# Products ahead of a norm for two outputs together and then one by one, and a shorter batch in the convolution's last projection

## The chip, the cores and the metric

The kernel runs on one core of a Trainium2 chip. The metric is the device time of one execution in microseconds (us). Engines are named as in the profile: PE is TensorE (matmuls; PEld its weight loads), DVE is VectorE, ACT is ScalarE, POOL is GpSimd, SP issues most of the DMAs.

## What is computed

A two-layer transformer block (first differential attention, then a gated short convolution as mixers, each followed by a gated feed-forward) and then a second block (a state-space branch, a pooling branch, a mixture of experts), on 256 tokens of width 1024 in 32-bit floats. What matters here is this pattern, which comes three times in the stretch that the change touches:

```python
h = rmsnorm(x, g) * (1.0 + scale) + shift      # x * rsqrt(mean(x*x) + eps) * g, then modulate
y = h @ w_in                                    # short conv: 3 parts; feed-forward: 2 parts; block 2: many
...
x = x + gate * (inner @ w_out)
mod = silu(c) @ ada_w + ada_b                   # shift, scale, gate of each layer ("adaLN")
```

The short convolution computes `(b_gate * conv(c_gate * u)) @ w_out` with `b_gate, c_gate, u = split(h @ w_in)`.

## The kernel before, in words

**Layout.** Activations lie with channels on the partitions: x is eight tiles of 128 channels by 256 tokens. An output of 128 channels is the sum over k of eight (or, behind a feed-forward, 22) products of 128 by 128 weight tiles with 128 by 256 activation tiles. Every operand is split in a high and a low half (`wh`, `wl` for weights, `hh`, `hl` for h), and each product is three matmuls (`mm3`, L277 to L282). A *unit* is eight weight tiles, 24 matmuls.

**Weights.** `Stream` loads them in order, two units a DMA (`fill`, L125), into a ring of four. `split_to` (L137) turns a unit into its halves: `wh` by a copy on ScalarE (L146), `wl` by a subtraction on VectorE (`lows`, L134), in a ring of five buffers; a buffer comes free when TensorE has used its unit up. `take(n, ahead)` (L175) hands out n tiles; for each unit that it starts it splits up to `ahead` units further on (3 where nothing is given) and calls `background`. `more(n)` splits up to n units from the present place.

**Order.** The program is written out in order by hand; each engine runs its instructions in the order in which the program issues them and waits for the others by semaphores. What is issued first on ScalarE or VectorE goes first there, ready or not.

**Background.** The modulation vectors are sums on VectorE, one instruction of 128 by 1024 for each 128 entries (`ada`, L395), from a queue of 128. `background` (L248) adds `bg_pace` (0.7, in the convolution's projections 0.25) to a counter at each unit and runs one sum for each whole number; while `hold` is set it does nothing. `need(key)` (L256) runs what is left up to a certain part at once.

**Residual.** `residual` (L886) computes the eight outputs of a projection; for each, VectorE adds it to x (L910), and `after` issues the square of x on ScalarE for the norm's sum (`sumsq_step`, L332; GpSimd adds the squares up) and, ahead of a raw entry, the split of A times x (`Raw.split`, on ScalarE and VectorE, L930 and L931). Outputs named in `done` were computed before, together, by `together` (L781): for the convolution's last projection four (L1131).

**Products ahead of the norm.** A norm multiplies a token's column by one number, so products with x can run before that number is known. `Raw` (L916) does this for the first outputs of the next stage; two more columns carry the shift. `Raw.run` (L942) goes through the eight k with all the outputs side by side: after the first k it sums the squares on TensorE (`total`, L351) and issues the chain of small VectorE instructions for the reciprocal root (`rstd`); after the third it turns it into rows (matmul L953) and copies them on ScalarE (`rows_s`, L956). The rest of the k follow, and then `modulated` (L971), which makes h for all other outputs by `norm_apply` (L371): for each k a VectorE instruction (`na`, L379), a ScalarE copy (`hh`, L380) and a VectorE subtraction (`hl`, L383). The raw outputs are finished by `lift` (L963).

It is used three times: at the convolution (three outputs, called from L1075), at the second feed-forward (four, L1008, after the convolution's last projection) and at the second block (four, L1201). There `dt_products` (L1179) runs small products at each k beside it, two streams of squares are summed (L1156 and L1157), and after it a list of steps written by hand (L1524) sets the order: lifts, splits, convolution steps, and `cb` (L1343), a product of two of the results.

Of the kernel before, what the change touches and what calls it, by code (L numbers as in the profile page):

```python
# [8 lines left out]
F32 = mybir.dt.float32  # L9
# [8 lines left out]
P = 128  # L18
T = 256
D = 1024  # L20
KD = 8
# [86 lines left out]
class Stream:  # L108
# [51 lines left out]
    def more(self, n, defer=False):  # L160

        self.fill(self.pos // 8 // 2 + self.ring)
        self.split_to(self.pos // 8 + n, defer)
# [74 lines left out]
class Builder:  # L238
# [93 lines left out]
    def sumsq_step(self, ms, xk, k, tag="rp_a", **kw):  # L332

        nc = self.nc
        sq = self.wk.tile([P, T], F32, tag=tag if k == 0 else "sq", name="sq", bufs=2)
        if k == 0:
            self.acc[tag] = sq
        nc.scalar.activation(sq, xk, AF.Square, **kw)  # L338
        if 0 < k < KD - 2:
            nc.gpsimd.tensor_tensor(self.acc[tag], self.acc[tag], sq, op=ALU.add)  # L340
        if k == KD - 2:
            self.acc[tag, 1] = sq
        if k == KD - 1:
            self.totals.append((ms, (self.acc[tag], self.acc[tag, 1], sq)))
# [80 lines left out]
def build(ctx, tc, ap):  # L425
    b = Builder(ctx, tc, ap)
# [24 lines left out]
    st = b.st = Stream(b, ap["ws"], ap["ws"].shape[0], ST, 5, 3)  # L451
# [103 lines left out]
    raw = ms[:, 16:16 + 4 * KD].rearrange("p (n a) -> p n a", a=4)  # L555
    rps = b.aux.tile([P, 512], F32, tag="aux", name="rows")

    def sums(src):

        acc = b.wk.tile([P, T], F32, tag="rp_a", name="acc", bufs=2)  # L560
        nc.scalar.activation(acc, src[0], AF.Square)
        for k in ks[1:]:
            sq = b.wk.tile([P, T], F32, tag="sq", name="sq", bufs=2)
            nc.scalar.activation(sq, src[k], AF.Square)
            if k < KD - 1:
                nc.vector.tensor_tensor(acc, acc, sq, op=ALU.add)
        return acc, sq
# [46 lines left out]
    for n in ks:  # L614
        w = st.raw()
# [68 lines left out]
    for n in range(8):  # L684
        w = st.take(KD)
        ps = b.ps.tile([P, 2, T], F32, tag="ps", name="ps_k") if n else \
# [10 lines left out]
    lo_, _ = VEC["lam"]  # L697
# [48 lines left out]
    for n in range(4):  # L746
        pss = [b.ps.tile([P, 2, T], F32, tag="ps", name="ps_v") for _ in range(2)]
        for half in range(2):
            wh, wl, _ = st.take(8)[0]
            wh = wh.rearrange("p (k a) c -> p k (a c)", a=2)  # L750
            wl = wl.rearrange("p (k a) c -> p k (a c)", a=2)
            for kk in range(4):
                k = half * 4 + kk
                for tt in range(4):
                    o = pss[tt // 2][:, tt % 2]
# [17 lines left out]
    def by_tiles(outs, xh, xl):  # L773

        w = st.take(KD * len(outs), 5 - len(outs))
        for k in range(KD):
            for i, o in enumerate(outs):
                b.mm3(o, w[i * KD + k], xh[:, k], xl[:, k], k == 0 and i % 2 == 0, k == KD - 1)
            yield

    def together(outs, xh, xl):  # L781
        for _ in by_tiles(outs, xh, xl):
            pass
        return outs
# [101 lines left out]
    def residual(ktiles, xh, xl, gate, sums, done=(), raw=None):  # L886


        pend = []

        def after():
            n = pend.pop(0)
            sums(n)
            if raw:
                raw.split(n)

        for n in range(KD):
            if n < len(done):
                ps = done[n]
            else:  # L900
                b.hold = raw is not None and n == KD - 1
                w = st.take(ktiles)
                ps = b.ps.tile([P, 512], F32, tag="ps", name="ps_r")[:, :T]
                for k in range(ktiles):
                    b.mm3(ps, w[k], xh[:, k], xl[:, k], k == 0, k == ktiles - 1)
                while pend:
                    after()
                if raw and n == KD - 1:
                    st.more(4)
            nc.vector.scalar_tensor_tensor(x[:, n], ps, gate[:, n:n + 1], x[:, n], op0=ALU.mult, op1=ALU.add)  # L910
            pend.append(n)
        after()
        if not raw:
            st.more(4, True)

    class Raw:  # L916
# [14 lines left out]
            nc.vector.scalar_tensor_tensor(self.L[:, n, :T], x[:, n], A, self.H[:, n, :T], op0=ALU.mult, op1=ALU.subtract)  # L931

        def steps(self, outs, more):
            w = st.take(KD * len(outs), 0)
            for k in range(KD):
                if more:
                    more(k)
                for i, o in enumerate(outs):
                    b.mm3(o[:, :T + 2], w[i * KD + k], self.H[:, k], self.L[:, k], k == 0, k == KD - 1)
                yield  # L940

        def run(self, rstd, outs, more=None):  # L942

            go = self.steps(outs, more)
            next(go)
            b.total()
            r = self.r = rstd()
            st.more(5 - len(outs))
            next(go)
            next(go)  # L950
            rows = self.rows_ps = b.aux.tile([P, 512], F32, tag="aux", name="rows")
            for tt in range(2):
                nc.tensor.matmul(rows[:, tt * P:(tt + 1) * P], lhsT=r[:, 2 * tt:2 * tt + 1].to_broadcast([P, P]),  # L953
                                 rhs=ident, start=(tt == 0), stop=True, skip_group_check=True)
            self.rows = b.wk.tile([P, T], F32, tag="rp_b", name="rows_s", bufs=2)
            nc.scalar.activation(self.rows, rows[:, :T], AF.Copy)  # L956
            for _ in go:
                pass
            hh, hl = modulated(self.rows, self.A, self.B)
            b.hold = False  # L960
            return hh, hl
# [9 lines left out]
    def modulated(rows, A, B):  # L971
        hh = hpool.tile([P, KD, T], F32R, tag="hh", name="hh", bufs=1)
        hl = hpool.tile([P, KD, T], F32R, tag="hl", name="hl", bufs=1)
        b.norm_apply([x[:, k] for k in ks], rows, A, B, [hh[:, k] for k in ks], [hl[:, k] for k in ks])
        return hh, hl
# [5 lines left out]

    ms = b.new_ms()
    residual(KD, oH, oL, mod(0, 2), lambda n: b.sumsq_step(ms, x[:, n], n), wo_out)
    b.ada_last = ada2
    b.ada_bufs = [w for w in b.ada_bufs if w is not ada2]
# [18 lines left out]
    def ffn(i, ms, sums, after, raw=None):  # L1004
# [39 lines left out]
        for j in range(2, KFF):  # L1044
            ps = b.ps.tile([P, 512], F32, tag="ps", name="ps_f")
            for a in range(2):
                w = st.take(KD)
                next(steps, None)
                project(w, ps[:, a * T:(a + 1) * T], hh, hl, a == 0)
                next(steps, None)  # L1050
            steps = glu(j, ps)
        for _ in steps:
            pass
        b.need((key, 5))
        u = after()
        residual(KFF, gH, gL, mod(i, 5), sums, (), u)
        fs.close()
        return u
# [19 lines left out]
    rH = cvp.tile([P, KD, T], F32R, name="rH")  # L1078
    rL = cvp.tile([P, KD, T], F32R, name="rL")
# [35 lines left out]
    for i in range(1, KD):  # L1115
        ps = b.ps.tile([P, 512], F32, tag="ps", name="ps_cu")
        pb = b.ps.tile([P, 512], F32, tag="ps", name="ps_b")
        for j, o in enumerate((ps[:, :T], ps[:, T:], pb[:, :T])):
            w = st.take(KD)
            next(steps, None)  # L1120
            project(w, o, hh, hl, j != 1)
            next(steps, None)
        for _ in steps:
            pass
        steps = conv(i, ps, pb)
# [2 lines left out]
        pass  # L1128
    b.bg_pace = 0.7
    b.need(("L1", 2))  # L1130
    pss = [b.ps.tile([P, 2, T], F32, tag="ps", name="ps_so") for _ in range(2)]  # L1131
    so_out = together([pss[i // 2][:, i % 2] for i in range(4)], rH, rL)
    ms2 = b.new_ms()
    raw3 = Raw(*ffn_in(1), yp, "yL")
    residual(KD, rH, rL, mod(1, 2), lambda n: b.sumsq_step(ms2, x[:, n], n), so_out, raw3)
    cs_.close()

# [278 lines left out]
    po, _ = CST["pinv"]  # L1416
# [272 lines left out]
    ro, _ = VEC["router_bias_2"]  # L1689
# [49 lines left out]
    for q in range(4):  # L1739
# [4 lines left out]
        for i in range(2):  # L1744
            k = 2 * q + i
# [7 lines left out]
    ro, _ = VEC["router_bias_2"]  # L1753
# [110 lines left out]
    ps = []  # L1864
# [281 lines left out]
    for i in range(4):  # L2146
        y, o, f = piece(i)
# [5 lines left out]
    for i, eng in ((0, nc.sync), (1, nc.scalar), (3, nc.sync), (2, nc.scalar)):  # L2153
        y, o, f = piece(i)
# [158 lines left out]
```

## Time and profile before

| | us |
|---|---|
| three runs | 1561.92, 1558.98, 1562.48 (median 1561.92) |
| the profiled execution | 1554.01 |
| its span in the trace | 1552.2 |
| TensorE busy in it | 1480.8 (95%), mean granted clock 0.988 |
| VectorE busy | 987.8 (64%) |
| ScalarE busy | 669.0 (43%) |

Times in a timeline are from the span's start. A timeline line gives start, duration, engine, line and operation, output and inputs by tile name, shape, and how many instructions it merges; in brackets stands how long the engine was idle before it and who ended that. Instructions overlap with their neighbours, so the distance of two starts, and not the duration, is what one costs in a row.

### The profile page before, as it was taken

The page shows a single profiled execution, that of the slowest core. Times are in us where ns is not written, and L with a number is a line of the kernel's source. Part 1 is how long each engine was busy: PE and PEld are TensorE (multiplying, and loading weights), DVE is VectorE, ACT ScalarE, POOL GpSimd, SP SyncE. Part 2 cuts the span into 40 slices and gives each one's busy share as a digit, 9 for nine tenths or more (in the row PEclk, how much of TensorE's full clock was granted, in tenths as well). Part 3 has the DMA queues.
Part 4 walks back from the last instruction along what each step waited for, and adds up shares of the span by engine and source line. Part 5 has one row for each costly group of instructions (what it writes and reads, how often), then busy time and mean ns, then how long its engine had stood idle before and what let it go on. Part 6 is the DMA issues. An engine that isn't in the chain of part 4 may idle for free. (4 is left out here: it accounts for less than half of the span.)

```text
span 1552.2 us, 28284 instructions
## 1 busy us (share of the span) xinstructions
PE 1480.8 (95%) x11184; PEld 1185.0 (76%) x11184; DVE 987.8 (64%) x1850; ACT 669.0 (43%) x1175; POOL 276.2 (18%) x439
## 2 busy tenths in 40 slices
PE   6999888999999999999899999999999999999996
PEld 5788578999999899999899998999634444444432
DVE  3698767888888789887888877465423333323332
ACT  3524554544455454454677765443322222222222
POOL 0170560000100100021067667001100000000000
PEclk9999999999999899999999999999999999999998
DMA  9678224987957569786444544667489999999995
GB/s 388 224 247 284 103 73 186 347 326 292 352 197 250 191 231 355 297 312 236 145 167 153 190 164 154 237 249 324 164 310 414 420 419 421 420 419 420 421 420 210
DMA packets 71429, 431.93 MB, mean 278 GB/s; under 512 B 8176, under 2 KB 8688, under 8 KB 28416
## 3 DMA queue, kind: packets, MB, share of 16 engines
q1 hardware_dynamic: 68656, 422.77, 71.0%
q0 software_dynamic: 1344, 4.80, 0.8%
q10 hardware_dynamic: 1296, 2.55, 0.5%
q8 instruction: 88, 1.44, 0.4%
q14 instruction: 45, 0.37, 0.1%
HBM read 429.01 MB, written 1.08 MB: 277 GB/s over the span
## 5 line engine op out<-in xcount | busy, mean ns | idle before, releaser
L134 DVE TENSOR_TENSOR wl<-st,wh 128x1024 fp32r<-128x1024 f32 x294 | 364.7, 1249 | 74.5 <-ACT wh L146 74.0
L146 ACT ACTIVATE wh<-st 128x1024 fp32r<-128x1024 f32 x294 | 306.2, 1055 | 113.2 <-PE ps_r L281 45.2
L280 PE MATMUL ps_f<-hh,wh 128*128 128x256 f32 x672 | 189.6, 282 | 2.5 <-ACT hh L380 2.1
L282 PE MATMUL ps_f<-hh,wl 128*128 128x256 f32 x672 | 189.5, 282 | 0.7 <-DVE wl L134 0.7
L281 PE MATMUL ps_f<-hl,wh 128*128 128x256 f32 x672 | 189.4, 282 | 0.1
L395 DVE SCALAR_TENSOR_TENSOR ada<-ada,crow 128x1024 f32<-128x1024 f32 x128 | 164.8, 1295 | 18.3 <-DMA ada<-in_ada 18.3
L340 POOL TENSOR_TENSOR sq<-sq 128x256 f32<-128x256 f32 x30 | 40.5, 1356 | 575.6 <-ACT sq L338 575.2
L280 PEld LDWEIGHTS ps_f<-hh,wh 128*128 128x128 f32 x672 | 127.6, 190 | 2.9 <-ACT hh L380 2.3
L282 PEld LDWEIGHTS ps_f<-hh,wl 128*128 128x128 f32 x672 | 127.5, 190 | 1.0 <-DVE wl L134 1.0
L281 PEld LDWEIGHTS ps_f<-hl,wh 128*128 128x128 f32 x672 | 127.6, 190 | 0.3 <-DVE hl L383 0.3
L280 PE MATMUL ps_ssd<-hh,wh 128*128 128x256 f32 x352 | 101.4, 288 | 0.0
L280 PE MATMUL ps_r<-gH,wh 128*128 128x256 f32 x352 | 98.7, 280 | 0.0
L281 PE MATMUL ps_r<-gL,wh 128*128 128x256 f32 x352 | 98.7, 280 | 0.0
L282 PE MATMUL ps_r<-gH,wl 128*128 128x256 f32 x352 | 98.7, 280 | 0.0
L282 PE MATMUL ps_ssd<-hh,wl 128*128 128x256 f32 x352 | 98.6, 280 | 0.0
L281 PE MATMUL ps_ssd<-hl,wh 128*128 128x256 f32 x352 | 98.6, 280 | 0.0
L1817 DVE TENSOR_SCALAR xb<-gtp,A,mod 128x256 f32<-128x256 f32 (+2 forms) x52 | 27.4, 526 | 111.5 <-ACT xb L1815 111.3
L1815 ACT ACTIVATE xb<-gtp,mod,A 128x256 f32<-128x256 f32 (+2 forms) x52 | 28.6, 551 | 118.6 <-PE gtp L1835 118.4
L1805 POOL TENSOR_TENSOR WG<-G,pwq 128x256 f32<-128x256 f32 (+2 forms) x24 | 14.1, 608 | 366.4 <-DVE G L1801 366.4
L274 ACT ACTIVATE oH<-wr 128x512 fp32r<-128x512 f32 (+2 forms) x53 | 33.4, 630 | 95.2 <-DVE wr L2093 82.6
L1835 PEld LDWEIGHTS gtp<-G,utH 128*128 128x128 f32 x208 | 39.2, 189 | 45.9 <-DVE xb L1817 19.7
L280 PEld LDWEIGHTS ps_ssd<-hh,wh 128*128 128x128 f32 x352 | 66.3, 188 | 1.0 <-issue 1.0
(616 smaller groups left out, 4156.0 us busy)
## 6 DMA issues: line engine op xcount, KB each, us to landing
st<-in_ws SPq DMA_DIRECT2D x151, 1024.0 KB, 6.0
ada<-in_ada SPq DMA_DIRECT2D x128, 512.0 KB, 5.0
w<-in_we SPq DMA_DIRECT2D x40, 1024.0 KB, 19.8
w_st<-in_we SPq DMA_DIRECT2D x40, 1024.0 KB, 19.8
w_y<-in_we SPq DMA_DIRECT2D x32, 1024.0 KB, 19.8
w_ut<-in_we SPq DMA_DIRECT2D x30, 1024.0 KB, 19.8
w_h<-in_we SPq DMA_DIRECT2D x21, 1024.0 KB, 19.8
x<-in_we SPq DMA_DIRECT2D x10, 1024.0 KB, 19.8
```

The source lines that it names most:

```text
L134: self.b.nc.vector.tensor_tensor(lo.rearrange("p a c -> p (a c)"), w, h.rearrange("p a c -> p (a c)"), op=ALU.subtract)
L146: nc.scalar.activation(h.rearrange("p a c -> p (a c)"), w, AF.Copy)
L274: self.nc.scalar.activation(h, src, AF.Copy)
L280: nc.tensor.matmul(out, lhsT=h[:, k], rhs=xh, start=start, stop=False, skip_group_check=True)
L281: nc.tensor.matmul(out, lhsT=h[:, k], rhs=xl, start=False, stop=False, skip_group_check=True)
L282: nc.tensor.matmul(out, lhsT=lo[:, k], rhs=xh, start=False, stop=stop, skip_group_check=True)
L340: nc.gpsimd.tensor_tensor(self.acc[tag], self.acc[tag], sq, op=ALU.add)
L395: self.nc.vector.scalar_tensor_tensor(junk, w, 1.0, crow, op0=ALU.mult, op1=ALU.mult, accum_out=dst[:, j:j + 1])
L1805: nc.gpsimd.tensor_tensor(cut(WG, tt), cut(G, tt), ws_[:, tt][:, :, None].to_broadcast([P, n, c]), op=ALU.mult)
L1815: nc.scalar.activation(out[:, k, :n], tp[:, i, :n], AF.Identity, scale=A, bias=B)
L1817: nc.vector.tensor_scalar(out[:, k, :n], tp[:, i, :n], A, B, op0=ALU.mult, op1=ALU.add)
L1835: nc.tensor.matmul(tp[:, i, :n], lhsT=hl_[:, tt, k * P:(k + 1) * P], rhs=G[:, tt, :n], start=(i == 0 and tt == 0 and hl_ is utH), stop=(tt ...
```

## The change

Products ahead of the norm are done for the first two outputs together and then for each other output alone; the squares are summed after the third k of the pair and the rows made after its last. `dt_products` runs with the pair. The pair takes its weights with two units ahead and each single output with three. The convolution's last projection does two outputs together instead of four, and from its fifth output on no background sums run (in the other residuals ahead of a raw entry still from the eighth on). The call that split four units ahead of the last x is gone, and so is the one after the `rstd`. The square of the seventh tile of x goes into a buffer of the tag `na`.

```diff
--- before.py
+++ after.py
@@ -332,7 +332,8 @@
     def sumsq_step(self, ms, xk, k, tag="rp_a", **kw):
 
         nc = self.nc
-        sq = self.wk.tile([P, T], F32, tag=tag if k == 0 else "sq", name="sq", bufs=2)
+        kept = k == KD - 2
+        sq = self.wk.tile([P, T], F32, tag="na" if kept else "sq" if k else tag, name="sq", bufs=3 if kept else 2)
         if k == 0:
             self.acc[tag] = sq
         nc.scalar.activation(sq, xk, AF.Square, **kw)
@@ -898,15 +899,13 @@
             if n < len(done):
                 ps = done[n]
             else:
-                b.hold = raw is not None and n == KD - 1
+                b.hold = raw is not None and n >= (KD - 1 if ktiles > KD else 4)
                 w = st.take(ktiles)
                 ps = b.ps.tile([P, 512], F32, tag="ps", name="ps_r")[:, :T]
                 for k in range(ktiles):
                     b.mm3(ps, w[k], xh[:, k], xl[:, k], k == 0, k == ktiles - 1)
                 while pend:
                     after()
-                if raw and n == KD - 1:
-                    st.more(4)
             nc.vector.scalar_tensor_tensor(x[:, n], ps, gate[:, n:n + 1], x[:, n], op0=ALU.mult, op1=ALU.add)
             pend.append(n)
         after()
@@ -931,23 +930,25 @@
             nc.vector.scalar_tensor_tensor(self.L[:, n, :T], x[:, n], A, self.H[:, n, :T], op0=ALU.mult, op1=ALU.subtract)
 
         def steps(self, outs, more):
-            w = st.take(KD * len(outs), 0)
-            for k in range(KD):
-                if more:
-                    more(k)
-                for i, o in enumerate(outs):
-                    b.mm3(o[:, :T + 2], w[i * KD + k], self.H[:, k], self.L[:, k], k == 0, k == KD - 1)
-                yield
+
+            for g in (outs[:2], *[[o] for o in outs[2:]]):
+                w = st.take(KD * len(g), 4 - len(g))
+                for k in range(KD):
+                    if more and g[0] is outs[0]:
+                        more(k)
+                    for i, o in enumerate(g):
+                        b.mm3(o[:, :T + 2], w[i * KD + k], self.H[:, k], self.L[:, k], k == 0, k == KD - 1)
+                    yield
 
         def run(self, rstd, outs, more=None):
 
             go = self.steps(outs, more)
-            next(go)
+            for _ in range(3):
+                next(go)
             b.total()
             r = self.r = rstd()
-            st.more(5 - len(outs))
-            next(go)
-            next(go)
+            for _ in range(KD - 3):
+                next(go)
             rows = self.rows_ps = b.aux.tile([P, 512], F32, tag="aux", name="rows")
             for tt in range(2):
                 nc.tensor.matmul(rows[:, tt * P:(tt + 1) * P], lhsT=r[:, 2 * tt:2 * tt + 1].to_broadcast([P, P]),
@@ -1128,8 +1129,8 @@
         pass
     b.bg_pace = 0.7
     b.need(("L1", 2))
-    pss = [b.ps.tile([P, 2, T], F32, tag="ps", name="ps_so") for _ in range(2)]
-    so_out = together([pss[i // 2][:, i % 2] for i in range(4)], rH, rL)
+    pss = [b.ps.tile([P, 2, T], F32, tag="ps", name="ps_so")]
+    so_out = together([pss[0][:, i] for i in range(2)], rH, rL)
     ms2 = b.new_ms()
     raw3 = Raw(*ffn_in(1), yp, "yL")
     residual(KD, rH, rL, mod(1, 2), lambda n: b.sumsq_step(ms2, x[:, n], n), so_out, raw3)
```

## Rows read from the trace of the kernel before

**Rows 1.** The page: TensorE's busy time, and the high halves of the weights on ScalarE

```profile
PE 1480.8 (95%) x11184; PEld 1185.0 (76%) x11184; DVE 987.8 (64%) x1850; ACT 669.0 (43%) x1175; POOL 276.2 (18%) x439
...
L146 ACT ACTIVATE wh<-st 128x1024 fp32r<-128x1024 f32 x294 | 306.2, 1055 | 113.2 <-PE ps_r L281 45.2
```

**Rows 2.** Timeline, TensorE, conv entry: start us, us, engine line op out<-in

```profile
430.71 0.28 PE L280 MATMUL ps_cu<-u,wh 128*128 128x258 f32 x1
...
431.80 1.40 PE L351 MATMUL ms<-ones,sq 128*128 128x2 f32 x12
...
433.05 0.36 PE L280 MATMUL ps_cu<-u,wh 128*128 128x258 f32 x1
...
435.29 0.61 PE L953 MATMUL rows<-csts,rs_r 128*128 128x128 f32 x4
...
441.13 0.28 PE L280 MATMUL ps_cu<-hh,wh 128*128 128x256 f32 x1
...
443.95 0.28 PE L280 MATMUL ps_cu<-hh,wh 128*128 128x256 f32 x1
```

**Rows 3.** Timeline, TensorE, second feed-forward entry

```profile
523.85 0.28 PE L280 MATMUL ps_f<-u,wh 128*128 128x258 f32 x1
...
526.44 0.39 PE L282 MATMUL ps_f<-u,wl 128*128 128x258 f32 x1 [1.82 <-DVE wl L134]
...
550.77 0.28 PE L280 MATMUL ps_f<-hh,wh 128*128 128x256 f32 x1
```

**Rows 4.** Busy time in stretches: PE, PEld, DVE, ACT, POOL, PEclk, DMA, GB/s

```profile
524.00:527.00 3.00, 1.01 (x7) 0.60 (x5) 3.00 (x4) 1.66 (x3) 1.65 (x2) 1.00 1.00 418
...
533.00:537.00 4.00, 4.00 (x20) 4.00 (x21) 2.71 (x14) 0.02 (x1) 0.00 (x0) 0.50 0.83 339
...
757.00:761.00 4.00, 1.58 (x14) 1.38 (x13) 3.86 (x9) 3.97 (x7) 0.00 (x0) 1.00 0.39 125
```

**Rows 5.** Timeline, VectorE, second feed-forward entry

```profile
522.77 1.21 DVE L395 SCALAR_TENSOR_TENSOR ada<-ada,crow 128x1024 f32<-128x1024 f32 x1
...
525.17 1.21 DVE L134 TENSOR_TENSOR wl<-st,wh 128x1024 fp32r<-128x1024 f32 x1
```

**Rows 6.** Timeline, ScalarE, block-2 entry

```profile
727.62 0.42 ACT L338 ACTIVATE sq<-x 128x256 f32<-128x256 f32 x1 [5.18 <-PE ms L351]
```

**Rows 7.** Timeline, TensorE, block-2 entry

```profile
724.15 0.19 PE L1185 MATMUL ps_c<-wd,u 128*1 128x64 f32 x1
...
725.05 0.37 PE L280 MATMUL ps_ssd<-u,wh 128*128 128x258 f32 x1
...
728.09 0.27 PE L351 MATMUL ms<-ones,sq 128*128 128x2 f32 x1 [0.56 <-ACT sq L338]
...
760.85 0.48 PE L1343 MATMUL cb<-sb 128*128 128x256 f32 x1 [2.42 <-ACT sb L1283]
```

**Rows 8.** Timeline, ScalarE, conv entry

```profile
435.94 0.38 ACT L956 ACTIVATE rows_s<-rows 128x256 f32<-128x256 f32 x1 [2.68 <-PE rows L953]
```

**Rows 9.** Timeline, VectorE, conv entry

```profile
434.75 1.23 DVE L134 TENSOR_TENSOR wl<-st,wh 128x1024 fp32r<-128x1024 f32 x1
436.36 1.28 DVE L379 SCALAR_TENSOR_TENSOR na<-x,A,rows_s 128x256 f32<-128x256 f32 x3 [0.38 <-ACT rows_s L956]
...
442.13 1.27 DVE L383 SCALAR_TENSOR_TENSOR hl<-na,mod,hh 128x256 fp32r<-128x256 f32 x3
...
443.75 2.36 DVE L134 TENSOR_TENSOR wl<-st,wh 128x1024 fp32r<-128x1024 f32 x2 [0.31 <-ACT wh L146]
```

**Rows 10.** Timeline, VectorE, block-2 entry

```profile
735.37 1.28 DVE L379 SCALAR_TENSOR_TENSOR na<-x,A,rows_s 128x256 f32<-128x256 f32 x3 [1.90 <-ACT rows_s L956]
...
743.30 0.42 DVE L967 TENSOR_TENSOR lift<-ps_ssd,rows_s 128x256 f32<-128x256 f32 x1 [0.81 <-PE ps_ssd L282]
...
752.52 1.23 DVE L134 TENSOR_TENSOR wl<-st,wh 128x1024 fp32r<-128x1024 f32 x1 [0.88 <-ACT wh L146]
```

**Rows 11.** Timeline, VectorE, last adaLN sum

```profile
712.48 1.22 DVE L395 SCALAR_TENSOR_TENSOR ada<-ada,crow 128x1024 f32<-128x1024 f32 x1
```
## The prediction

> **What bounds the kernel now.** Start with the page: TensorE is busy for 95% of the span [rows 1], so a change can only win where TensorE waits or runs at its lower clock, and it loses wherever it makes a new wait. So the second view is the timeline of TensorE around the three places where products run ahead of a norm. I call them the conv entry (three outputs, from 430.71 us), the second feed-forward entry (four, from 523.85) and the block-2 entry (four, from 724.15). A unit is eight weight tiles: 24 matmuls, 2.82 us at full clock (441.13 to 443.95) [rows 2].
>
> At the conv entry TensorE hardly waits. At the second feed-forward entry it stalls, first on a low weight half [rows 3], and in the windows view the granted clock falls from 1.00 to 0.50, that is 1.2 instead of 2.4 GHz, after TensorE had been busy for 1.01 us of three [rows 4]. VectorE, busy for all of those three, is the late one: an adaLN sum (1.2 us) and splits stand ahead of what TensorE wants [rows 5]. At the block-2 entry ScalarE's last square waits 5.18 us until TensorE has read an older square out of the same buffer [rows 6], and TensorE then waits 0.56 us for it [rows 7]. Further on it waits 2.42 us, from 758.43, before `cb` [rows 7], at the end of a long row of VectorE work.
>
> **What each step is worth.** All shifts are against the profiled execution.
>
> *Second feed-forward entry, gain.* Four outputs at once free all their weight buffers at once, so the splits behind them come in a bunch, with adaLN sums between. The change does two outputs at once, then one each 2.82 us. Per unit VectorE then has a low half (1.14 us, two in 2.36), a residual step and a split of x (instructions of the form that follows itself every 0.40, three in 1.27) [rows 9], 1.94 us in all, and from the fifth output on no sums: it keeps up, and the first products start at 523.85 as now, but without the stall. From that start: 18 matmuls (2.12 us), 12 small matmuls of the squares (1.25, from 431.80 to 433.05 [rows 2]), 30 matmuls (3.53), so the row matmul R is at 530.75; the rstd (done within 1.7 us, from 433.05 to the low half at 434.75 [rows 2, 9]) is hidden by the 30. Then comes the new price. The remaining outputs call for weights with three units ahead, after the row copy and before the normalised tiles in program order: units U+4, U+5 and U+6, each 1.05 us on ScalarE [rows 1] and 1.14 on VectorE. ScalarE's row copy starts 0.65 after R [rows 2, 8], takes 0.35, the first high half 1.05, and three low halves 3.42: the first normalised tile (`na`) starts at R + 5.47 = 536.2. From there to the last low half of h are 7.04 us (436.36 to 443.40) [rows 9], so 543.25. TensorE has its two single outputs until R + 0.37 + 5.64 = 536.8, is then paced by VectorE (0.92 us for each three matmuls), ends its first unit with h at 543.6 and, as its splits are done by then, the second at 546.4. Now, the second unit has 21 matmuls left at 550.77 [rows 3] and ends at 553.2. **Gain 6.8 us.**
>
> *Conv entry, loss.* By the same steps from 430.71: R = 430.71 + 2.12 + 1.25 + 3.53 = 437.6 (now 435.29). With three outputs one single output is left, so two splits stand ahead of the norm: `na` at R + 4.33 = 441.95, now 436.36 [rows 9]. Now one low half stands there, at 434.75, in the time in which VectorE waits for the rows anyway; the two next come behind h, at 443.75 [rows 9]. TensorE has the single output until 440.8 and then waits. h is complete 7.04 after 441.95, at 449.0, and the first unit with h ends 0.35 later instead of at 443.95 [rows 2]: **loss 5.4 us**. The work behind it is TensorE's, without slack. What this does to the clock the trace of before can't show here; the nearest row is the stall above, where a wait of 1.8 us and a sparse stretch led to 0.50 [rows 3, 4]. Here the wait is about 2 us and then three matmuls come per 0.92 us, so I take it to fall: 20 matmuls started in 4.0 us at 0.50 [rows 4] where 34 would have, 1.6 us lost. Ends: 0 and 2.5. **Loss 1.6 us.**
>
> *Block-2 entry, loss.* The kept square in a buffer of its own ends the wait of [rows 6]: the last squares start 0.1 us after the last x, about 2.7 earlier, and the two squares are done before TensorE wants them. But the row matmul comes later. From 724.15: 0.90 for the constants' products [rows 7], three steps of six matmuls (0.70) with two small groups between (0.45 each, an estimate: half of the 0.90), 0.8 for the second constants' product and its wait (an estimate: a high half of 1.05 us on ScalarE stands ahead of what it reads), 24 small matmuls (2.5, twice the 12): 731.3. Five steps of 1.15 give R = 737.1. Three splits: `na` at R + 5.47 = 742.6, now 735.37 [rows 10], complete at 749.6 instead of 742.4. Then one more sum: the change passes over three background calls at a pace of 0.7 (four taken together and three singles become two and two), 2.1 sums that come later. The last sum now runs at 712.48 [rows 11], one call ahead of the hold of the feed-forward's last output, so one sum is left over and is forced between h and the first lift: 1.25 us with its add. The first lift thus starts at 751.0 instead of 743.30: +7.7. From that lift to `cb` VectorE works nearly without a break (one idle time of 0.88 [rows 10]), so `cb` moves by 6.5 to 7.7. I take 7.2. TensorE's own work would be late by 2.8 only (single outputs until 743.1, a paced unit until 749.95, four units until 761.2 where they now end at 758.4) and waits for the rest. **Loss 7.2 us**, between 2.8, if `cb` had another cover, and 8.5.
>
> *At nothing.* The removed call for four units split one more unit ahead of the last x; it now follows the last split of x, 1.05 us on ScalarE and 1.14 on VectorE, hidden by the 18 matmuls ahead of the squares; without that cover the rstd is 0.3 late, inside the 30 matmuls. Weight DMAs: the same ones, a tile is asked for as both its halves are split, which is earlier here; SP and POOL get nothing new. The kept square changes no wait at the other entries, where the last square waits for x.
>
> Sum: 5.4 + 1.6 + 7.2 − 6.8 = **+7.4 us**. The profiled execution took 1554.0, so it would take 1561.4. It lies 7.9 below the median shown, 1561.9; I put the same shift on the median: **1569.3**.
>
> The windows row over 757 to 761 shows the clock still at 1.00 with a wait of 2.42 us inside [rows 4], and I charge a fall only at the conv entry. The Trainium skill (TensorE: Matmul & The Clock Gate, "A second HAM failure mode: psum-queue depth-cycling") says that frequent short idle times between groups of matmuls are enough to make the clock swing; by that the two other paced units would lose the clock too and the sum be about +10.6. That is the second rival; its price stands there from rows.
>
> **The rivals.** *Faster.* The splits find their way into VectorE's idle time between rstd and rows, so that only the row copy stands ahead of the norm. This hangs on one point, whether ScalarE's row copy really stands ahead of the high halves in its queue. Then `na` is at R + 1.07 everywhere: conv entry +2.1, block 2 +2.9, second feed-forward −10.8 (first h unit paced no more, second ends at 542.4): −5.8, 1556.1. For it: now one split does run in that gap (434.75) [rows 9]. Against it: the next two run behind h, where the program has them, and the change has them behind the row copy.
>
> *Clock in all three paced stretches.* 1.6 twice more: +10.6, 1572.5. For it the row 533 to 537, against it the row 757 to 761 [rows 4].
>
> *No gain at the second feed-forward entry.* VectorE's lateness stays, for instance because postponed sums are forced at its head: +14.2, 1576.1. Against it: the part needed there is complete before, by the count of calls.
>
> *Little.* The clock doesn't fall and `cb` isn't what block 2 waits for: 5.4 + 2.8 − 6.8 = +1.4, 1563.3. Against it: the wait before `cb` is already there [rows 7].
>
> **How the numbers follow.** Forecast 0.52, clock everywhere 0.13, no gain 0.07, little 0.13, faster 0.15. A measurement of this kernel tells about 0.2% (3.1 us) from no change. The forecast, the clock and the lost gain lie above it (0.72), and of "little" 0.03 does too with the conv entry's clock: slower 0.75, same 0.10, faster 0.15. Range 1559.5 to 1576.0 (−2.4 to +14.1): it takes in the bounds above and leaves out most of the faster case and the far end. The slower cases alone: 1565 to 1576.
>
> **What would show it.** In the trace after: at each entry two (conv) or three `wh` directly behind `rows_s` on ScalarE and as many `wl` ahead of the first `na`; `na` 4.3 or 5.5 us behind the row matmul; the first h unit starting each three matmuls 0.92 apart; at 524 to 531 no wait for `wl` and the clock at 1.00; one `ada` between the last `hl` and the first lift of block 2; `cb` with a wait of 6 to 7 us. The prediction is wrong if `na` follows the row copy at once, or if the second feed-forward entry still waits for `wl`.

## The result, and the profile after

The changed kernel took 1567.71 us (median of 19 runs, 1560.79 to 1572.81), the kernel before 1558.98 beside it (19 runs, 1551.37 to 1562.48). The ratio is **1.0061 [1.0047, 1.0075]**: 9.5 us slower (7.3 to 11.7), more than the 0.2% that a measurement of this kernel can tell. The prediction had +7.4 and 1569.3.

The profiled execution of the changed kernel took 1572.81 us (span 1571.0), 5 above its median, as that of before lay below its own. So spans are not compared here, but stretches, each from its own start. The conv entry starts 6.88 us later than before already, ahead of the three places that the change bears on; the end of the block-2 stretch (the first `yps`, the product with the state) comes 16.48 later; **9.6 us** lie between, about as many as the ratio shows.

| from the first product with x | before | after | difference |
|---|---|---|---|
| conv entry: to the row matmul R | 4.58 | 7.09 | +2.5 |
| conv entry: to the second unit with h | 13.24 | 19.54 | +6.3 |
| conv entry: to the second feed-forward entry | 93.14 | 98.39 | +5.3 |
| second feed-forward: to R | 14.40 | 7.09 | −7.3 |
| second feed-forward: to the third unit with h | 29.42 | 24.79 | −4.6 |
| second feed-forward: to the block-2 entry | 200.30 | 193.75 | −6.6 |
| block 2: to R | 10.16 | 16.37 | +6.2 |
| block 2: to `cb` | 36.70 | 46.69 | +10.0 |
| block 2: to the first `yps` | 61.88 | 72.78 | +10.9 |

Of the last row of each of the first two stretches 1.0 and 1.9 us are no effect of the change: behind the units named, TensorE has nothing but dense matmuls in both kernels, and one execution runs them 1% faster than another (see the last section).

The page of the changed kernel, busy time of the engines and the high halves, against [rows 1]:

```profile
PE 1494.1 (95%) x11184; PEld 1194.7 (76%) x11184; DVE 987.9 (63%) x1850; ACT 669.8 (43%) x1175; POOL 274.3 (17%) x439
...
L146 ACT ACTIVATE wh<-st 128x1024 fp32r<-128x1024 f32 x294 | 306.2, 1055 | 104.7 <-PE ps_r L281 41.2
```

TensorE has the same 11184 matmuls and is busy 13.3 us longer, while VectorE and ScalarE have what they had. That fits its mean granted clock, 0.982 in this execution and 0.988 in that of before. Where the clock stood low, the windows of the changed kernel show (columns as in [rows 4]):

```profile
450.00:454.00 4.00, 3.72 (x12) 2.90 (x13) 3.86 (x10) 2.37 (x6) 0.00 (x0) 0.53 0.80 262
...
553.00:559.40 6.40, 6.40 (x27) 5.99 (x28) 5.18 (x13) 2.95 (x6) 0.00 (x0) 0.50 0.01 3
...
733.70:735.70 2.00, 2.00 (x20) 2.00 (x20) 0.52 (x3) 0.00 (x0) 0.00 (x0) 1.00 0.53 70
735.70:737.70 2.00, 2.00 (x17) 2.00 (x17) 0.50 (x4) 0.00 (x0) 0.00 (x0) 0.82 0.88 373
737.70:743.70 6.00, 6.00 (x30) 6.00 (x29) 1.39 (x12) 0.00 (x0) 0.00 (x0) 0.50 0.08 30
...
752.60:757.00 4.40, 2.95 (x14) 1.94 (x14) 4.22 (x11) 2.78 (x6) 0.00 (x0) 1.00 0.45 192
...
776.40:781.30 4.90, 4.88 (x21) 4.70 (x22) 4.80 (x22) 0.37 (x1) 0.00 (x0) 0.50 0.68 249
```

The sixth number behind the length of the stretch is the clock. It is 0.50 (1.2 GHz), or a little more where the stretch takes in the fall, in four places: in the paced unit at the conv entry (the first unit with h, where TensorE runs only as fast as VectorE delivers h), in the one at the second feed-forward entry, behind the squares of block 2, and behind the wait before `cb`. The paced unit of block 2 (752.60) ran at 1.00.

The timeline of ScalarE in the changed kernel, against [rows 6, 8]:

```profile
445.32 0.38 ACT L957 ACTIVATE rows_s<-rows 128x256 f32<-128x256 f32 x1 [5.18 <-PE rows L954]
445.60 2.00 ACT L146 ACTIVATE wh<-st 128x1024 fp32r<-128x1024 f32 x2
...
543.72 0.39 ACT L957 ACTIVATE rows_s<-rows 128x256 f32<-128x256 f32 x1 [5.19 <-PE rows L954]
544.00 2.96 ACT L146 ACTIVATE wh<-st 128x1024 fp32r<-128x1024 f32 x3
...
730.50 0.42 ACT L339 ACTIVATE sq<-x 128x256 f32<-128x256 f32 x1 [4.16 <-DVE x L909]
...
746.74 0.38 ACT L957 ACTIVATE rows_s<-rows 128x256 f32<-128x256 f32 x1 [13.97 <-PE rows L954]
747.02 2.96 ACT L146 ACTIVATE wh<-st 128x1024 fp32r<-128x1024 f32 x3
```

ScalarE stands idle for 5 to 14 us at the row copy, with two or three high halves queued behind it that need nothing of the norm. They are issued behind the row copy and so wait with it. By the program the first of them could have run in that time: four units are split by then, and the ring has five buffers. The others get their buffers only as TensorE uses up the pair, just before R. The square at 730.50 waits for x alone now; the wait of [rows 6] is gone.

VectorE, the same kernel, against [rows 9, 10]:

```profile
446.69 2.36 DVE L134 TENSOR_TENSOR wl<-st,wh 128x1024 fp32r<-128x1024 f32 x2 [3.78 <-ACT wh L146]
448.97 1.27 DVE L380 SCALAR_TENSOR_TENSOR na<-x,A,rows_s 128x256 f32<-128x256 f32 x3
...
545.08 3.50 DVE L134 TENSOR_TENSOR wl<-st,wh 128x1024 fp32r<-128x1024 f32 x3 [3.79 <-ACT wh L146]
548.50 1.27 DVE L380 SCALAR_TENSOR_TENSOR na<-x,A,rows_s 128x256 f32<-128x256 f32 x3
...
748.11 3.50 DVE L134 TENSOR_TENSOR wl<-st,wh 128x1024 fp32r<-128x1024 f32 x3 [9.02 <-ACT wh L146]
751.52 1.27 DVE L380 SCALAR_TENSOR_TENSOR na<-x,A,rows_s 128x256 f32<-128x256 f32 x3
...
757.29 1.27 DVE L384 SCALAR_TENSOR_TENSOR hl<-na,mod,hh 128x256 fp32r<-128x256 f32 x3
758.48 1.22 DVE L396 SCALAR_TENSOR_TENSOR ada<-ada,crow 128x1024 f32<-128x1024 f32 x1
...
759.91 0.42 DVE L968 TENSOR_TENSOR lift<-ps_ssd,rows_s 128x256 f32<-128x256 f32 x1
```

It waits for the first high half, makes two or three low halves, and only then starts on the norm: 4.29, 5.43 and 5.42 us behind R.

TensorE, the same kernel, against [rows 2, 3, 7]:

```profile
444.68 0.49 PE L954 MATMUL rows<-csts,rs_r 128*128 128x128 f32 x3
...
450.04 0.41 PE L280 MATMUL ps_cu<-hh,wh 128*128 128x256 f32 x1 [1.89 <-ACT hh L381]
450.69 0.58 PE L281 MATMUL ps_cu<-hl,wh 128*128 128x256 f32 x1 [0.24 <-DVE hl L384]
...
451.60 0.58 PE L281 MATMUL ps_cu<-hl,wh 128*128 128x256 f32 x1
...
452.52 0.58 PE L281 MATMUL ps_cu<-hl,wh 128*128 128x256 f32 x1
...
543.07 0.60 PE L954 MATMUL rows<-csts,rs_r 128*128 128x128 f32 x4
...
734.45 2.80 PE L352 MATMUL ms<-ones,sq 128*128 128x2 f32 x24
737.12 0.40 PE L1199 MATMUL ps_dt<-wd,u 128*128 128x64 f32 x1
...
776.42 1.22 PE L1344 MATMUL cb<-sb 128*128 128x256 f32 x2 [5.91 <-ACT sb L1284]
```

The wait at 450.04, and the products with `hl` that follow each other every 0.92 us (450.69, 451.60, 452.52), show the paced unit; the 24 narrow matmuls start at 734.45, the next instruction 2.67 later; the wait before `cb` has grown from 2.42 [rows 7] to 5.91.

### The profile page after: what moved, and what is told of

It is laid out like the page before. It is cut to its first block, busy times and chain, and to the rows that moved or that the text cites. A ratio compares the mean times of both kernels' runs of the same rounds, so it can differ in the third digit from the quotient of the medians.

```text
span 1571.0 us, 28280 instructions
## 1 busy us (share of the span) xinstructions
PE 1494.1 (95%) x11184; PEld 1194.7 (76%) x11184; DVE 987.9 (63%) x1850; ACT 669.8 (43%) x1175; POOL 274.3 (17%) x439
## 5 line engine op out<-in xcount | busy, mean ns | idle before, releaser
L281 PEld LDWEIGHTS ps_ssd<-hl,wh 128*128 128x128 f32 x352 | 66.4, 189 | 3.0 <-DVE hl L384 3.0
```

The lines of the kernel that those rows point to most:

```text
L281: nc.tensor.matmul(out, lhsT=h[:, k], rhs=xl, start=False, stop=False, skip_group_check=True)
```

## The experiments

Ratios are to the kernel before, on the same chip. The stretches, in us from the first product with x, in one profiled execution of each:

| | conv: to second h unit | 2nd ffn: to R | 2nd ffn: to third h unit | block 2: to `yps` |
|---|---|---|---|---|
| before | 13.24 | 14.40 | 29.42 | 61.88 |
| changed | 19.54 | 7.09 | 24.79 | 72.78 |
| 1 splits before the rows | 16.11 | 7.09 | 22.09 | 71.41 |
| 2 pair order alone | 19.54 | 14.98 | 32.71 | 71.85 |
| 3 projection alone | 13.23 | 5.65 | 20.64 | 66.66 |
| 4 kept square alone | 13.26 | 14.76 | 29.74 | 61.21 |
| 5 projection and kept square | 13.24 | 5.67 | 20.70 | 61.28 |
| 6 as 5, one more sum | 13.24 | 6.46 | 21.47 | 61.15 |
| 7 as 5, squares spread | 13.23 | 5.67 | 20.70 | 63.86 |
| 8 hold alone | 13.24 | 12.33 | 27.31 | 65.03 |

Each row is one execution, so its stretches need not add up to what the ratio, from several runs, shows.

**1. The splits out of the norm's way.** The changed kernel, with one unit split behind the `rstd` and the others where the kernel before has them.

```diff
-                w = st.take(KD * len(g), 4 - len(g))
+                w = st.take(KD * len(g), 2 if len(g) == 2 else 0)
...
             r = self.r = rstd()
+            st.more(3)
```

> The changed kernel, but the split of the next unit (U+4) is asked for right behind the rstd, and the single outputs ask for none ahead; the others come behind the norm, as in the kernel before. Theory (the splits behind the row copy are what delays the norm): the first normalised tile 1.1 us behind the row matmul at all three entries instead of 4.3 to 5.5; conv entry 5 us shorter than in the changed kernel, second feed-forward entry 5 to 6, block 2 4 to 5: about 14 us faster than the changed kernel, ratio to the kernel before 0.996 to 0.998. Rival (the loss comes from the later row matmul and the clock, whatever stands between): less than 4 us of the loss comes back, ratio 1.003 or more.

Measured: 1558.17 us (10 runs), ratio 0.9997 [0.9971, 1.0023]: 9.5 us less than the changed kernel by the medians, 10 by the two ratios. ScalarE and VectorE of this kernel at the conv entry, in that order:

```profile
441.42 0.38 ACT L958 ACTIVATE rows_s<-rows 128x256 f32<-128x256 f32 x1 [4.25 <-PE rows L955]
442.36 1.31 ACT L381 ACTIVATE hh<-na,mod 128x256 fp32r<-128x256 f32 x3 [0.55 <-DVE na L380]
```

```profile
438.91 1.23 DVE L134 TENSOR_TENSOR wl<-st,wh 128x1024 fp32r<-128x1024 f32 x1
441.84 1.27 DVE L380 SCALAR_TENSOR_TENSOR na<-x,A,rows_s 128x256 f32<-128x256 f32 x3 [1.70 <-ACT rows_s L958]
```

Nothing stands between row copy and `hh` now, and `na` starts 1.06 us behind R (440.78) instead of 4.29. So the place of the splits in the program is what the changed kernel pays for: this one edit takes back all that it lost. It doesn't take back the 14 us that the theory had. The conv entry is still 2.9 us longer than before, as only one unit can run there between R and h and the next is paced. At the second feed-forward entry 2.7 us came back, and not 5 to 6, since the units that are now split behind the norm come late for the second unit with h. TensorE there:

```profile
547.71 0.38 PE L280 MATMUL ps_f<-hh,wh 128*128 128x256 f32 x1 [1.83 <-ACT wh L146]
...
548.97 0.38 PE L282 MATMUL ps_f<-hh,wl 128*128 128x256 f32 x1 [0.76 <-DVE wl L134]
```

And at block 2 the clock stood low for longer; windows of this kernel:

```profile
730.00:744.00 14.00, 14.00 (x66) 14.00 (x67) 3.20 (x16) 0.38 (x1) 0.00 (x0) 0.50 0.07 30
```

There R came at 19.60 us from the entry, later than in the changed kernel (16.37), though `na` then followed at once, and only 1.4 us came back. How much of the 10 us came back by way of the clock was not tried apart (see the last section).

**2. The pair order alone.** The kernel before with the new `steps` and `run`, and with the kept square, without which this order can't run. The core of the edit:

```diff
...
+            for g in (outs[:2], *[[o] for o in outs[2:]]):
+                w = st.take(KD * len(g), 4 - len(g))
...
```

> The kernel before with the products ahead of the norm in the new order (and the kept square, without which this order can't run), the convolution's last projection as before. Theory: conv entry +6, block 2 +9 (no sum is left over here), second feed-forward entry -1 to +1, since VectorE is as late there as before: +14 to +16 us, ratio about 1.0095. Rival (the pair itself, which needs two units at a time, gives the gain at the second feed-forward entry): -5 there, +10 us in all, ratio about 1.0065.

Measured: 1574.8 us (5 runs), ratio 1.0094 [1.0061, 1.0126]: 14.7 us slower. Conv entry +6.3, second feed-forward +3.3, block 2 +10.0. At the second feed-forward entry R comes no sooner than before (14.98), since four outputs of the projection still go together; so the new order by itself gains nothing in any of these stretches.

**3. The projection alone.** The kernel before with two outputs together and the sums held from the fifth output on; order and splits of the products ahead of the norm as before.

```diff
-                b.hold = raw is not None and n == KD - 1
+                b.hold = raw is not None and n >= (KD - 1 if ktiles > KD else 4)
...
-    pss = [b.ps.tile([P, 2, T], F32, tag="ps", name="ps_so") for _ in range(2)]
-    so_out = together([pss[i // 2][:, i % 2] for i in range(4)], rH, rL)
+    pss = [b.ps.tile([P, 2, T], F32, tag="ps", name="ps_so")]
+    so_out = together([pss[0][:, i] for i in range(2)], rH, rL)
```

> The kernel before with only the convolution's last projection changed (two outputs together, no sums from the fifth on). Theory: the stall at the second feed-forward entry goes, and with it the fall of the clock, 8 to 10 us; one left-over sum at block 2 costs 1.2 us: -8 us, ratio about 0.995. Rival (the gain needs the pair): 0 to -2 us, ratio above 0.998.

Measured: 1548.83 us (7 runs), ratio **0.9934 [0.9912, 0.9956]**: 10.3 us faster. The second feed-forward is 8.8 us shorter than before and 4.2 shorter than in the changed kernel, so the gain of the change lies in this part alone, and the pair order gives a part of it back. In this trace block 2 took 4.8 us longer than before: R came 14.27 us from its entry instead of 10.16, at a low clock, so the ratio shows more than these stretches add up to. A window of this kernel ahead of that R (731.64):

```profile
723.00:731.00 8.00, 8.00 (x36) 7.66 (x37) 3.76 (x19) 0.96 (x2) 0.00 (x0) 0.50 0.01 2
```

**4. The kept square alone.**

```diff
-        sq = self.wk.tile([P, T], F32, tag=tag if k == 0 else "sq", name="sq", bufs=2)
+        kept = k == KD - 2
+        sq = self.wk.tile([P, T], F32, tag="na" if kept else "sq" if k else tag, name="sq", bufs=3 if kept else 2)
```

> The kernel before with only the seventh square in a buffer of its own. Theory: ScalarE's wait of 5.2 us at block 2 goes, TensorE's row matmul comes 1.3 us earlier and so does the chain up to cb: -1 to -2 us, ratio about 0.999. Rival (hidden): the row matmul where it is, 0 us.

Measured: 1555.53 us (10 runs), ratio 0.9983 [0.9963, 1.0003]. In the trace R of block 2 comes at 9.44 instead of 10.16, so the wait of [rows 7] is gone and 0.7 us with it, about half of the 1.3 expected. The timing alone can't tell that from nothing.

**5. Projection and kept square.** Edits 3 and 4 together.

> The kernel before with the convolution's last projection changed and the kept square, the products ahead of the norm as before. Theory (the parts add up): the projection's gain of about 10 us and the kept square's of about 2: ratio 0.991 to 0.993. Rival (the kept square hides behind the left-over sum at block 2): as the projection alone, 0.9935 or more.

Measured: **1547.87 us** (6 runs), ratio 0.9933 [0.9908, 0.9958]. This beats both kernels; from experiment 3 it can't be told apart, and the ratio lies between the two that were expected. TensorE and then the windows of this kernel at the second feed-forward entry (525.80):

```profile
527.25 1.40 PE L352 MATMUL ms<-ones,sq 128*128 128x2 f32 x12
531.47 0.61 PE L954 MATMUL rows<-csts,rs_r 128*128 128x128 f32 x4
539.09 0.29 PE L280 MATMUL ps_f<-hh,wh 128*128 128x256 f32 x1
```

```profile
525.00:529.00 4.00, 4.00 (x37) 4.00 (x36) 2.71 (x7) 2.25 (x4) 0.00 (x0) 1.00 0.64 221
529.00:533.00 4.00, 4.00 (x35) 4.00 (x35) 2.90 (x15) 0.49 (x2) 0.00 (x0) 1.00 0.85 346
533.00:537.00 4.00, 4.00 (x36) 4.00 (x35) 3.86 (x11) 2.73 (x6) 0.00 (x0) 1.00 0.02 8
```

With four outputs side by side TensorE has work for 7.6 us between R and the first unit with h, nearly what VectorE's norm takes (`na` at 532.53, h complete 7.04 us later), so the first unit with h is not paced, and the clock stays at 1.00.

**6. Without the left-over sum.** As experiment 5, but the sums are held from the sixth output on, so that none is left for block 2.

```diff
-                b.hold = raw is not None and n >= (KD - 1 if ktiles > KD else 4)
+                b.hold = raw is not None and n >= (KD - 1 if ktiles > KD else 5)
```

> The same with sums held from the sixth output on instead of the fifth, so that one more background call counts and no sum is left over at block 2. Theory: no ada between the last hl and the first lift, cb 1.2 us earlier relative to the row matmul, nothing lost at the second feed-forward entry: 1 us below the run of the projection with the kept square. Rival (the sum in the projection makes VectorE late again): a wait for wl at the second feed-forward entry, 1 us or more above it.

Measured: 1549.05 us (7 runs), ratio 0.9933 [0.991, 0.9957], as experiment 5; by the ratios neither the 1 us less nor the 1 us more shows. From R of block 2 to `cb` it takes 26.56 us without and 26.55 with the sum between h and the first lift: there the sum is hidden. At the second feed-forward R comes 0.8 later for the sum that runs there: TensorE waits 0.53 us for a low half (at 532.52), the rival's sign in a small way.

**7. The squares of block 2 in two parts.** As experiment 5, with twelve of the 24 two-column matmuls behind the first k and twelve behind the second.

```diff
...
-            b.total()
+            b.total(1)
+            if b.totals:
+                next(go)
+                b.total()
```

> The projection with the kept square; at block 2 the 24 small matmuls of the squares are done as 12 behind the first k and 12 behind the second instead of 24 behind the first, so the rows come one k later. [...]

Measured: 1548.08 us (6 runs), ratio 0.9924 [0.9897, 0.9951]. The question was whether the clock, which stood low from these 24 matmuls on in some of the traces, stays up where their row is shorter. The mean granted clock over the runs is 0.9897, against 0.9895 in experiment 5, so no difference shows. But the experiment can't decide it: in the traced execution of experiment 5 there was no fall here to take away, as its window behind the first squares (from 721.7) shows:

```profile
723.00:729.00 6.00, 6.00 (x51) 5.79 (x51) 3.32 (x18) 0.00 (x0) 0.00 (x0) 1.00 0.06 18
```

In the trace of experiment 7 R comes 1.8 us later from the block-2 entry than in experiment 5, and the stretch to `yps` is 2.6 longer; the times of all runs don't show that.

**8. The hold alone.** The kernel before with the one line on `b.hold` of experiment 3; four outputs together as before.

> The kernel before with only the longer hold of the sums; four outputs together as before, so that one or two sums fewer run in the projection, and one is left over at block 2. Theory (two bunches make the stall, splits and sums): a third to a half of the projection's gain, -3 to -5 us, ratio about 0.9975. Rival (the sums alone make VectorE late): the whole gain, -9, ratio about 0.994; other rival (the splits alone): 0.

Measured: 1555.15 us (10 runs), ratio 0.9984 [0.9962, 1.0006]. The second feed-forward is 2.1 us shorter than before, a quarter of what experiment 3 gains there, where a third to a half was expected. TensorE and the windows of this kernel behind the entry at 525.81, against [rows 3, 4]:

```profile
526.93 0.39 PE L280 MATMUL ps_f<-u,wh 128*128 128x258 f32 x1 [0.23 <-ACT wh L146]
528.61 0.39 PE L282 MATMUL ps_f<-u,wl 128*128 128x258 f32 x1 [1.17 <-DVE wl L134]
529.33 0.39 PE L280 MATMUL ps_f<-u,wh 128*128 128x258 f32 x1 [0.34 <-ACT wh L146]
530.59 0.44 PE L282 MATMUL ps_f<-u,wl 128*128 128x258 f32 x1 [0.76 <-DVE wl L134]
```

```profile
533.00:537.00 4.00, 4.00 (x19) 4.00 (x20) 2.71 (x14) 0.00 (x0) 0.00 (x0) 0.50 0.74 301
```

Without the sums the stall is shorter (four waits of 0.23 to 1.17) but it is there, and the clock falls as before. With two outputs together as well (experiment 3) the stall is gone; by the program the buffers then come free a unit at a time from the third output on. Whether that would do without the hold was not run.

## Why the prediction was right

The direction, the mechanism and the range held. That the time came out so near is in part luck. The forecast of 1569.3 stands on a median of three runs, 1561.9; the 19 runs beside the changed kernel have 1558.98, which is 2.9 lower, and the shift was larger than forecast, by 1.3 in the medians and 2.1 in the ratio. The two offset each other. And of the terms, one charged the clock too much and two didn't charge it at all:

**Conv entry (predicted +5.4, and +1.6 for the clock).** R came 7.09 us from the entry (predicted 6.89), `na` 4.29 behind it (4.33), TensorE waited 1.89 (about 2), then ran three matmuls per 0.92, and the clock fell to 0.53 in these 4 us. The second unit with h starts 6.3 late, against 7.0. That the clock falls here was only taken from the stall in the trace of before; it did, but cost less: from `na` at 11.38 the steps lead to 18.8 us from the entry without it (7.04 to the end of h, 0.35 to the end of the first unit), and the unit came at 19.54. So the clock took 0.8 and not 1.6.

**Second feed-forward entry (predicted −6.8).** No wait for a low half, the clock at 1.00 up to R (535.00 to 539.00 and 543.00 to 549.57 both show 1.00), R at 7.09 (6.9), `na` at 12.52 (12.35): all as worked out. The step that failed is "ends its first unit with h at 543.6 and, as its splits are done by then, the second at 546.4", which charged no clock. The row 553.00 to 559.40 shows 0.50, and the second unit ended 24.79 us from the entry instead of 22.55: 2.24 late, 0.17 of it by `na` and the other 2.1 by the clock. The term is −4.6.

**Block 2 (predicted +7.2).** The last squares start 2.70 us earlier from the entry (0.77 instead of 3.47), as predicted. The 24 narrow matmuls ended 7.39 behind the entry (predicted 7.15). Then "Five steps of 1.15 give R = 737.1" failed: they took 8.98 instead of 5.75, at a clock of 0.50. Behind R all is as worked out: `na` at 5.42 (5.47), h complete 7.04 later (7.04), one sum between the last `hl` and the first lift, 1.35 us (1.4). `cb` came 10.0 later, with a wait of 5.91 (6 to 7); without the 3.2 of the clock that is 6.8, in the predicted 6.5 to 7.7. From `cb` to the first `yps` it took another 0.9 more than before; the row from 776.40, behind the longer wait, shows 0.50, a fall that the prediction didn't charge. The left-over sum delays the lift by its whole price, yet R to `cb` takes only 0.5 more than in experiment 2, which has none there (30.32 against 29.84).

**The clock.** By steps the profiled execution has +6.3 − 4.6 + 10.9 = 12.6, and less the 1.0 and 1.9 of the faster dense stretches 9.6. That this meets the 9.5 of the 19 runs is chance as far as one execution of each kernel can tell. In places where the forecast charged no clock it took some 6.2 here (2.1 at the second feed-forward, 3.2 and 0.9 at block 2), which with the 0.8 less at the conv entry leads from 7.4 to 12.6 within 0.2. The second rival (+10.6) has 3.2 for such places, so it isn't that rival in size. Nor is it in place: that one had the paced unit of block 2 at the low clock, and that unit ran at 1.00 (752.60 to 757.00). The Trainium skill (TensorE: Matmul & The Clock Gate, "A second HAM failure mode: psum-queue depth-cycling"), by which frequent short idle times between groups of matmuls make the clock swing, agrees with two of the three paced units and not with the third. The interval of the ratio (7.3 to 11.7) holds the forecast and the second rival alike, so the times don't decide between them; the clock differs between executions.

**The other rivals.** "Faster" hung on whether the row copy really stands ahead of the high halves in ScalarE's queue. It does (445.32, then 445.60), and experiment 1, with nothing there, shows what it is worth: 9.5 to 10 us, where the forecast and that rival lie 13.2 apart. "No gain at the second feed-forward entry" and "little" fell with the table: −4.6 there, and `cb` is what block 2 waits for.

## What to carry to other kernels

On an engine with an in-order queue, look at what is issued behind an instruction that waits for a late result: work that needs nothing of that result and stands behind it is lost time twice, first for the idle engine and then for the result's reader. Spreading a batch pays where its end makes a bunch for another engine (the projection, 10 us together with the hold, which alone gives a quarter of the stretch's gain); where the batch covers a wait (four outputs side by side ahead of a norm), spreading it takes the cover away. When a change has two parts, time each alone: here one gained 10 us and the other cost 15. Together they cost 9.5, more than the 4.4 that the two ratios add up to, though their intervals leave room for that.

## What the runs showed that was not expected

*The clock is a sum of its own.* The mean granted clock of the timed runs tells how long it stood at 0.50: the span times twice the clock's distance from 1. That is 57 us in the changed kernel (0.982, 19 runs), 46 in the one before (0.985, 23 runs), 43 in experiment 1 (0.986, 10 runs) and 33 in experiment 5 (0.9895, 6 runs). Half of such time is lost where TensorE is the bound: up to 5 us of the changed kernel's 9.5, up to 7 of the 10 that experiment 1 takes back, and up to 7 of the 10 by which experiment 5 is faster than before. Over the changed kernel's 19 runs clock and time correlate at −0.7. How much of each loss the clock made was not tried apart.

*The same work at two clocks.* Between the start of the 24 two-column matmuls of block 2 and R the clock stood low in the profiled executions of all three kernels with the pair order (changed, 1, 2). In the old order it did so in two of the three without the kept square (3 and 8, not before) and in none of the four with it (4 to 7). In the changed kernel TensorE had been busy for 2.00 of the 2.00 us ahead of the fall. That the kept square helps the clock there is suggested by this, by one execution of each, and not shown. What makes the clock fall there stays open.

*One percent between executions.* The same 59 us of dense matmuls in the second feed-forward (from its twentieth unit with h to its projection), at a clock of 1.00 throughout, took 59.13 us in the changed kernel's execution, 59.81 in that of before and 60.48 in that of experiment 5. Windows of the changed kernel:

```profile
608.64:667.77 59.13, 59.13 (x506) 59.13 (x505) 48.96 (x73) 27.77 (x41) 0.00 (x0) 1.00 0.87 315
```

It follows no edit, since the fastest kernel has the slowest stretch. So a stretch of two executions can be compared to about 1% of its dense part, and short stretches close to the change are worth more than long ones.
